# Order of the sums in the first quad of values, earlier rotary tables, and the first weight sums on VectorE

## The chip, the cores and the metric

The kernel runs on one core of a Trainium2 chip. The metric is the device time of one execution in microseconds (us); less is better. The engines are TensorE (PE: matmuls; PEld is its weight load), VectorE (DVE), ScalarE (ACT), GpSimd (POOL) and SyncE (SP, which here only issues loads). Each engine works through its own list of instructions in order and waits at an instruction until its operands and buffers are ready. DMA writes issued by POOL, and loads issued by SP, stand in those lists too.

## The reference, cut to what matters

A decoder block over 1024 positions of width 1024. The change touches its front, where the normed input is projected:

```
h    = rms_norm(x, pre_mix_norm)
proj = h @ w_in
xr, gr, q, k, v, gates = split(proj)
ang  = positions[..., None] * inv_freq          # rotary tables
cos, sin = cos(ang), sin(ang)
q = partial_rope(q, cos, sin) * 128 ** -0.5     # first 32 of 128 columns of each head
k = partial_rope(k, cos, sin)
...                                             # recurrence, dilated attention, merge, FFN
```

The values `v` come in three groups of 512 columns, since the attention has three dilations.

## The kernel before, in words

**Precision by splitting.** Every f32 operand of a product is split into a high part (ACT copies it to the matmul's type) and a low part (DVE subtracts the high part from the original). Three matmuls then stand for one: high x high, high x low, low x high (`mm3`, lines 133 to 135). A product can start when its high parts are there, and its second matmul wants the low part of the weight (values) or its third (projections).

**Seven products for eight.** Products are done as a 2 x 2 block scheme with seven block products (a "quad"). With a11, a12, a21, a22 the four blocks of a weight and b11, b12, b21, b22 those of the transposed input, sums and differences are formed first. For the input they are t1 = b12 - b11, t2 = b22 - t1, t4 = b21 - t2, t3 = b22 - b12 (`x_diffs`), for the weights s3 = a11 - a21, a21 + a22, that less a11, and a12 less that (`v_sums`).

**Stages in the front.** First, the values of group 0 (line 463). Then `v_quad(2, ...)`, the values of group 2, and `v_quad(1, ...)`, those of group 1, each with products b11, b21 (in `v_start`), t2, t1, b22, t3, t4 in that order, each of 48 matmuls of 128x256. `out` adds up two halves on DVE (`vs`) and POOL issues the write to `vd`. Then `rope_tables` makes cosine and sine on DVE (tiles `rot`) and ACT, and POOL issues six writes to `rtd`. Then `run_quads` does the projections: for the first two quads P1 and P2 (48 matmuls of 128x512), then the bodies, P6, P5, P3, P7, P4 of 12 matmuls each. `Quad.prep` forms the weight sums `sa` and `sb` with four operations on POOL (lines 267 to 270); ACT and DVE split them.

**What sets the order.** A scheduler orders each engine's list by the order in the program, by dependencies and by the ends that its own cost table gives; `tc.issue_after(i)` holds a block's instructions on an engine behind `i`. Buffers come from pools: the tag `x` has ten of [128, 1024] f32, for the input blocks and later for `vr`, `vp1`, `vu`, `vw` and `rot`; a tile gets one when its first write is placed, and waits for one to come free. t1, t3 and t4 are written over input blocks; t2 has two tiles of its own (`x2`). `wraw` has two buffers, `whi` and `wlo` three, `w0r` two.

Of the kernel before, what the change touches and what calls it, by code (L numbers as in the profile page):

```python
# [30 lines left out]
PRE1 = 2  # L31
# [31 lines left out]
def block(ctx, tc, a, out):  # L63
    nc = tc.nc
    V, A, G, T = nc.vector, nc.scalar, nc.gpsimd, nc.tensor
# [25 lines left out]
    def f(t):  # L91
        return t.bitcast(F32)
# [80 lines left out]
    last_dve = [None]  # L173
# [59 lines left out]
    class Quad:  # L233
# [25 lines left out]
            self.w = {}  # L259
            self.unit(self.raw(0, name), ("P1", "P2"))  # L260

        def prep(self):
            r0, r1 = self.raw(0), self.raw(1)
            lo_, hi_ = slice(0, 512), slice(512, 1024)
            sa = Quad.pool.tile([128, 1024], F32, name="sa")
            sb = Quad.pool.tile([128, 1024], F32, name="sb")
            G.tensor_add(sb[:, lo_], r1[:, lo_], r1[:, hi_])  # L267
            G.tensor_sub(sa[:, lo_], sb[:, lo_], r0[:, lo_])  # L268
            G.tensor_sub(sa[:, hi_], r0[:, lo_], r1[:, lo_])
            G.tensor_sub(sb[:, hi_], r0[:, hi_], sa[:, lo_])  # L270
            if self.w is None:
                self.w = {}
                self.unit(r0, ("P1", "P2"))
            self.unit(sa, ("P6", "P7"))
            self.unit(sb, ("P5", "P3"))
            h4 = Quad.pool.tile([128, 512], F32R, name="w4h", bufs=Quad.W4)
            l4 = Quad.pool.tile([128, 512], F32R, name="w4l")
            split(r1[:, hi_], h4, l4)
            self.w["P4"] = h4, l4
# [44 lines left out]
                self.done()  # L324
            yield

    def run_quads(quads, pre, tick=None):
        quads[0].prep()
        for j in range(pre):
            quads[j].first()  # L330
        for j, q in enumerate(quads):
            if j + 1 < len(quads):
                quads[j + 1].prep()
            for _ in q.body():
                if tick:
                    tick()
            if pre <= j + 1 < len(quads):
                quads[j + 1].head()
                if tick:
                    tick()  # L340
                quads[j + 1].first()
                if tick:
                    tick()
# [46 lines left out]
        return xf.tile(list(shape), F32, name=name, tag="x", bufs=10)  # L390

    X = [xq("x", (128, 2, 512)) for _ in range(10)]
    xt = dict(zip(((1, 2), (1, 3), (2, 0), (2, 1), (0, 0), (0, 1), (1, 0), (1, 1), (0, 2), (0, 3)), X))
    x2 = [xt[2, j] for j in range(2)]

    def pair(ts, j, h):

# [82 lines left out]
        for pr in range(2):  # L480
            G.dma_start(v_block(pr, 0, h), vs[:, :, 256 * pr:256 * pr + 256])

    def x_diffs(j):

        b11, b12, b21, b22 = (xt[h, 2 * u + j] for u in range(2) for h in range(2))
        V.tensor_sub(b11, b12, b11)
        V.tensor_sub(x2[j], b22, b11)
        V.tensor_sub(b21, b21, x2[j])
        V.tensor_sub(b12, b22, b12)

    for j in range(4):
        x_load(0, j)
# [61 lines left out]
    def x_split(n, src):  # L554
        for j in range(2):
            c = slice(2 * j, 2 * j + 2)
            A.activation(X1[n][0][:, c], src[j], AF.Copy)
            V.tensor_sub(X1[n][1][:, c], src[j], f(X1[n][0][:, c]))

    def x_sums(t, fl, x2c, X, names):  # L560

# [23 lines left out]
    def rope_tables():  # L585

        whole = [xq("rot") for _ in range(3)]
        pos_i, ang, nn, nh, tmp = (whole[i // 2][:, 384 * (i % 2):384 * (i % 2) + 384] for i in range(5))
        pos_i = pos_i.bitcast(I32)
        pos = a["positions"]  # L590
        A.dma_start(pos_i.rearrange("p (g n) -> p g n", g=NG),
                    bass.AP(tensor=pos.tensor, offset=pos.offset, ap=[[384, 8], [0, 16], [1, 384]]))
        V.tensor_copy(ang, pos_i)
        c1, c2, c3 = two_pi_parts()
        MAGIC = 1.5 * 2 ** 23
        V.tensor_scalar(ang, ang, cst[:, C_INV:C_INV + 1], None, op0=OP.mult)
        V.tensor_scalar(nn, ang, 1.0 / (2 * math.pi), MAGIC, op0=OP.mult, op1=OP.add)
        V.tensor_scalar(nn, nn, -MAGIC, None, op0=OP.add)
        V.tensor_scalar(nh, nn, 2.0 ** -11, MAGIC, op0=OP.mult, op1=OP.add)
        V.tensor_scalar(nh, nh, -MAGIC, 2.0 ** 11, op0=OP.add, op1=OP.mult)  # L600
        V.tensor_sub(tmp, nn, nh)
        for cc, parts in ((c1, (nh, tmp)), (c2, (nh, tmp)), (c3, (nn,))):
            for part in parts:
                V.scalar_tensor_tensor(ang, part, -cc, ang, op0=OP.mult, op1=OP.add)
        V.tensor_scalar(ang, ang, -math.pi, math.pi, op0=OP.max, op1=OP.min)
        V.scalar_tensor_tensor(tmp, ang, -1.0, ang, op0=OP.mult, op1=OP.min)
        V.tensor_scalar(tmp, tmp, math.pi / 2, None, op0=OP.add)
        A.activation(nn, ang, AF.Sin)
        A.activation(nh, tmp, AF.Sin)
        for s, src in ((0, nh), (1, nn)):  # L610
            for g in range(NG):
                G.dma_start(rtd[g, s].rearrange("f (b n) -> b f n", b=8), src[:, 128 * g:128 * g + 128])


    def v_mm(w, n):
        wh, wl = (t.rearrange("p (k n) -> p k n", n=256) for t in w)
        xh, xl = X1[n]
        bk = [ps("pv") for _ in range(2)]
        for q in range(4):
            mm3(bk[q // 2][:, 256 * (q % 2):256 * (q % 2) + 256],  # L620
                [(xh[:, k, 128 * q:128 * q + 128], xl[:, k, 128 * q:128 * q + 128], wh[:, k, :], wl[:, k, :])
                     for k in range(4)])
        return bk

    def v_split(src):
        hi = wp.tile([128, 1024], F32R, name="whi", tag="whi")
        lo = wp.tile([128, 1024], F32R, name="wlo", tag="wlo")
        A.activation(hi, src, AF.Copy)
        last_dve[0] = V.tensor_sub(lo, src, f(hi))
        return hi, lo  # L630
# [3 lines left out]

    def v_raw(g):
        r = [None] * 5
        for n in (2, 3, 0, 4, 1):
            if g == 1:
                r[n] = xq("vr")
            elif n in (2, 3):  # L640
                r[n] = w0p.tile([128, 1024], F32, name="vr", tag="w0r")
            elif n == 1:
                r[n] = xq("vr")
            else:
                r[n] = wraw()
            if n < 4:
                load(r[n], a["w_v"][n // 2, g - 1, n % 2])
        return r

    def v_sums(r):  # L650
        a11, a12, a21, a22, s3 = r
        V.tensor_sub(s3, a11, a21)
        V.tensor_add(a21, a21, a22)
        V.tensor_sub(a11, a21, a11)
        last_dve[0] = V.tensor_sub(a12, a12, a11)

    def v_quad(g, b, nxt, r, late=()):
        def add2(name, bk, x, y=None):
            if y is None:
                y = xq(name)  # L660
            for n, c in enumerate((LO, HI)):
                V.tensor_add(y[:, c], bk[n], x[:, c])
            return y

        def out(pr, u, bk, x):
            t = vp.tile([128, 4, 256], F32, name="vs")
            add2(None, bk, x, t.rearrange("p q n -> p (q n)"))
            G.dma_start(vd[pr, g, 512 * u:512 * u + 512].rearrange("(q p) n -> p q n", p=128), t)

        a11, a12, a21, a22, s3 = r  # L670
        p1 = xq("vp1")
        for n, c in enumerate((LO, HI)):
            A.activation(p1[:, c], b[0][n], AF.Copy)
        out(0, 0, b[1], p1)
        late = list(late)

        def split_and(src):
            w = v_split(src)
            if late:
                late.pop(0)()  # L680
            return w

        u2 = add2("vu", v_mm(split_and(a11), "t2"), p1)
        w = add2("vw", v_mm(split_and(a21), "t1"), u2)
        out(0, 1, v_mm(split_and(a12), "b22"), w)
        bk = v_mm(v_split(s3), "t3")
        out(1, 1, bk, w)
        v = add2("vw", bk, u2)
        b2 = v_mm(v_split(a22), "t4")
        if nxt:  # L690
            nb = v_start(nxt)
        out(1, 0, b2, v)
        return nb if nxt else None

    b = v_start(2)
    r = v_raw(2)
    v_sums(r)
    x_diffs(0)
    x_diffs(1)
    x_split("t2", x2)  # L700
    put(1, 2)
    put(1, 3)
    def x_late(n, x):
        def go():
            with tc.issue_after(last_dve[0].ins):
                x_split(n, x)

        return go

    b = v_quad(2, b, 1, r, (x_late("t1", [xt[0, 0], xt[0, 1]]), x_late("t3", [xt[1, 0], xt[1, 1]]),  # L710
                            x_late("t4", [xt[0, 2], xt[0, 3]])))
    r = v_raw(1)
    v_sums(r)
    v_quad(1, b, None, r)
    rope_tables()


    kinds = {n: dp.tile([8, 128, S], F32, name=n + "d") for n in ("xr", "gr", "gl", "ga")}
# [370 lines left out]
        todo.setdefault(c, []).append((yl_weights, (nb,)))  # L1089
    for n, (fn, args) in enumerate(EARLYA):  # L1090
        todo.setdefault(fn, []).append((after, args))
    run_quads(q1, PRE1, tick)
    assert not todo
    fctx.close()
    tctx.close()
# [509 lines left out]
```

## Time and profile before

| | before |
|---|---|
| runs (3) | 1737.4, 1739.75, 1740.69 us; median 1739.75 |
| profiled execution | 1737.8 us, of which the span from first to last instruction 1736.0 |
| PE busy | 1676.3 us, 97% of the span |
| DVE, ACT, POOL busy | 65%, 42%, 40% |
| mean granted TensorE clock | 0.982 of full speed |

PE is nearly always busy, so the time is set by its work and by the few places where it waits or where its clock is lower. Matmuls overlap, and their ends are modelled, so a matmul's row of 0.28 us doesn't mean that the next starts 0.28 us later; progress is read from the starts, or from a count over a stretch.

### The profile page before, as it was taken

Reading aid. Unit: us, or ns where it says so; the run is one execution under the profiler, and the core shown is the slowest. Engines: PE = TensorE matmul, PEld = TensorE weight load, DVE = VectorE, ACT = ScalarE, POOL = GpSimd, SP = SyncE. Lnnn points to the kernel's source line nnn. Section 1 sums busy time; section 2 is a strip of 40 time slices with the busy share of each in tenths; the row PEclk is TensorE's granted clock in tenths of the full one; section 3 lists DMA queues with packets and bytes.
Section 4 is the critical chain, followed back from the end, with each engine's and each line's share of the span. In section 5 each row is a group of like instructions: output and inputs, shape, how many; then the busy total and the mean of one; then the engine's idle time right before and its main releaser. Section 6 shows DMA issues by size and latency. Waiting matters only on the chain.

```text
span 1736.0 us, 21088 instructions
## 1 busy us (share of the span) xinstructions
PE 1676.3 (97%) x7748; PEld 1376.8 (79%) x7748; DVE 1121.0 (65%) x1591; ACT 728.4 (42%) x1130; POOL 693.2 (40%) x644
## 2 busy tenths in 40 slices
PE   9999999999999999989999999799999999999996
PEld 7897888787877887868888787678888888788885
DVE  7956577778887766554433678755554555659658
ACT  6423367564555532564441445323222222345343
POOL 2003454554445533133334205576566666400103
PEclk9999999999999999999999999899999999999998
DMA  8233433343333564683519742133222222475353
GB/s 322 85 123 123 146 128 130 131 149 118 128 133 134 167 206 156 229 317 135 195 50 359 245 147 73 61 123 126 103 91 103 92 96 105 160 255 191 109 188 121
DMA packets 95919, 262.70 MB, mean 151 GB/s; under 512 B 13768, under 2 KB 22120, under 8 KB 94408
## 3 DMA queue, kind: packets, MB, share of 16 engines
q1 hardware_dynamic: 70352, 182.49, 31.2%
q0 software_dynamic: 20352, 76.21, 11.6%
q10 hardware_dynamic: 5112, 2.66, 0.5%
q8 instruction: 61, 1.00, 0.2%
q14 instruction: 42, 0.34, 0.1%
HBM read 180.86 MB, written 80.35 MB: 150 GB/s over the span
## 4 chain that ended last, share of the span: by engine, by line
PE 77%; DVE 10%; DMA 4%; issue 4%; POOL 3%; ACT 3%; SPq 0%; ACTq 0%; DVEq 0%; POOLq 0%
PE pq L135 15%; PE pq L134 15%; PE pq L133 15%; PE pd L1351 4%; PE pd L1352 4%; PE pd L1350 4%; PE py L135 2%; PE py L133 2%; PE py L134 2%; PE pv L463 2%; PE po L1033 2%; PE pv L134 1%; PE pv L135 1%; DMA rsn<-rtd 1%; PE pv L133 1%
## 5 line engine op out<-in xcount | busy, mean ns | idle before, releaser
L133 PE MATMUL pq<-hth,whi 128*128 128x512 f32 x448 | 179.3, 400 | 2.7 <-ACT whi L98 2.7
L135 PE MATMUL pq<-hth,wlo 128*128 128x512 f32 x448 | 178.5, 399 | 3.1 <-DVE wlo L99 3.1
L134 PE MATMUL pq<-htl,whi 128*128 128x512 f32 x448 | 180.5, 403 | 0.0
L267 POOL TENSOR_TENSOR sb<-wraw 128x512 f32<-128x512 f32 x50 | 70.9, 1418 | 168.3 <-DMA wraw<-in_w_fg 92.1
L98 ACT ACTIVATE whi<-sa 128x1024 fp32r<-128x1024 f32 x50 | 52.9, 1059 | 198.6 <-PE pq L134 139.4
L1351 PE MATMUL pd<-fbl,fah 128*128 128x512 f32 x304 | 119.6, 394 | 4.5 <-DVE fbl L99 4.5
L1352 PE MATMUL pd<-fbh,fal 128*128 128x512 f32 x304 | 119.7, 394 | 0.0
L1350 PE MATMUL pd<-fbh,fah 128*128 128x512 f32 x304 | 119.4, 393 | 0.0
L99 DVE TENSOR_TENSOR wlo<-wraw,whi 128x1024 fp32r<-128x1024 f32 x67 | 97.5, 1456 | 23.6 <-ACT whi L98 20.8
L98 ACT ACTIVATE whi<-wraw 128x1024 fp32r<-128x1024 f32 x67 | 70.7, 1056 | 90.8 <-PE pq L134 26.3
L309 DVE TENSOR_TENSOR uw<-pq,uw 128x512 f32<-128x512 f32 x100 | 68.4, 684 | 57.6 <-PE pq L135 56.8
L133 PEld LDWEIGHTS pq<-hth,whi 128*128 128x128 f32 x448 | 85.8, 191 | 24.7 <-ACT whi L98 3.2
L135 PEld LDWEIGHTS pq<-hth,wlo 128*128 128x128 f32 x448 | 85.5, 191 | 24.3 <-DVE wlo L99 3.8
L134 PEld LDWEIGHTS pq<-htl,whi 128*128 128x128 f32 x448 | 85.7, 191 | 20.3
L1424 POOL TENSOR_TENSOR y<-y,gpf 128x512 f32<-128x512 f32 x16 | 26.2, 1663 | 186.0 <-ACT fah L98 109.7
L99 DVE TENSOR_TENSOR wlo<-sa,whi 128x1024 fp32r<-128x1024 f32 x50 | 70.1, 1402 | 27.7 <-ACT whi L98 27.7
L728 DVE TENSOR_TENSOR fb<-pq,uw 128x512 f32<-128x512 f32 x84 | 67.8, 807 | 30.6 <-PE pq L135 30.3
L1256 POOL TENSOR_TENSOR fo<-fo,ut 128x512 f32<-128x512 f32 x44 | 60.6, 1381 | 66.4 <-DVE ut L1255 66.4
L98 ACT ACTIVATE fah<-ar 128x1024 fp32r<-128x1024 f32 (+1 forms) x41 | 40.8, 995 | 98.6 <-PE pd L1351 76.5
L99 DVE TENSOR_TENSOR fal<-ar,fah 128x1024 fp32r<-128x1024 f32 (+1 forms) x41 | 49.3, 1203 | 48.7 <-ACT fah L98 48.6
L268 POOL TENSOR_TENSOR sa<-sb,wraw 128x512 f32<-128x512 f32 x50 | 80.2, 1604 | 0.0
L133 PE MATMUL pq<-t1h,whi 128*128 128x512 f32 x200 | 79.4, 397 | 0.5 <-ACT whi L98 0.5
(541 smaller groups left out, 4946.9 us busy)
## 6 DMA issues: line engine op xcount, KB each, us to landing
ar<-fd SPq DMA_DIRECT2D x35, 512.0 KB
qkd<-fb POOLq DMA_DIRECT2D x24, 512.0 KB, 3.6
qk<-qkd SPq DMA_DIRECT2D x24, 512.0 KB
wraw<-in_w_fg SPq DMA_DIRECT2D x24, 512.0 KB
wraw<-in_w_fu SPq DMA_DIRECT2D x24, 512.0 KB
fd<-fo POOLq DMA_DIRECT2D x11, 1024.0 KB, 4.3
wd<-in_w_dn SPq DMA_DIRECT2D x21, 512.0 KB
fd<-fs POOLq DMA_DIRECT2D x11, 768.0 KB, 5.6
```

Of the source, the lines that this page charges most:

```text
L98: A.activation(hi, src, AF.Copy)
L99: (le or V).tensor_sub(lo, src, f(hi))
L133: T.matmul(o, lh, rh, start=(first and i == 0), stop=False)
L134: T.matmul(o, lh, rl, start=False, stop=False)
L135: T.matmul(o, ll, rh, start=False, stop=(last and i == n - 1))
L267: G.tensor_add(sb[:, lo_], r1[:, lo_], r1[:, hi_])
L268: G.tensor_sub(sa[:, lo_], sb[:, lo_], r0[:, lo_])
L309: V.tensor_add(y, bank, x)
L728: V.tensor_add(o, half_in(bank, g), half_in(add, g))
L1350: T.matmul(o, ah[:, ts], bh, start=(i == 0), stop=False)
L1351: T.matmul(o, ah[:, ts], bl, start=False, stop=False)
L1352: T.matmul(o, al[:, ts], bh, start=False, stop=(i == NP - 1))
```

## The change

In the first quad of values, `x_diff` and `v_sums` now run in the order in which the products want them: t1 and t2, then the weight sums for the first two products, splits of t2 and of a11, of t1, and then t3; the last weight sum (`v_sum4`, a12) and t4 come during the quad. The raw blocks are loaded in the order a21, a11, a22, a12. Two small memsets write one column of t2's tiles at the start, so that they get their buffers there. `rope_tables` stands ahead of the last quad of values, and its six writes are issued by SP (cosine) and ACT (sine) instead of POOL. `run_quads` gets `V`, so that the first projection quad's four sums run on DVE.

```diff
-        def prep(self):
+        def prep(self, first=None):
...
-            G.tensor_add(sb[:, lo_], r1[:, lo_], r1[:, hi_])
-            G.tensor_sub(sa[:, lo_], sb[:, lo_], r0[:, lo_])
-            G.tensor_sub(sa[:, hi_], r0[:, lo_], r1[:, lo_])
-            G.tensor_sub(sb[:, hi_], r0[:, hi_], sa[:, lo_])
+            E = first or G
+            E.tensor_add(sb[:, lo_], r1[:, lo_], r1[:, hi_])
+            E.tensor_sub(sa[:, lo_], sb[:, lo_], r0[:, lo_])
+            E.tensor_sub(sa[:, hi_], r0[:, lo_], r1[:, lo_])
+            E.tensor_sub(sb[:, hi_], r0[:, hi_], sa[:, lo_])
...
-    xt = dict(zip(((1, 2), (1, 3), (2, 0), (2, 1), (0, 0), (0, 1), (1, 0), (1, 1), (0, 2), (0, 3)), X))
+    xt = dict(zip(((0, 0), (0, 1), (1, 2), (1, 3), (2, 0), (2, 1), (1, 0), (1, 1), (0, 2), (0, 3)), X))
     x2 = [xt[2, j] for j in range(2)]
+    for x in x2:
+        V.memset(x[:, 0, 0:1], 0.0)
...
-    def x_diffs(j):
...
+    def x_diff(n):
+
+        for j in range(2):
+            b11, b12, b21, b22 = (xt[h, 2 * u + j] for u in range(2) for h in range(2))
+            o, p, q = dict(t1=(b11, b12, b11), t2=(x2[j], b22, b11), t4=(b21, b21, x2[j]), t3=(b12, b22, b12))[n]
+            last_dve[0] = V.tensor_sub(o, p, q)
...
-                G.dma_start(rtd[g, s].rearrange("f (b n) -> b f n", b=8), src[:, 128 * g:128 * g + 128])
+                (A if s else nc.sync).dma_start(rtd[g, s].rearrange("f (b n) -> b f n", b=8), src[:, 128 * g:128 * g + 128])
...
-        for n in (2, 3, 0, 4, 1):
+        for n in (2, 0, 3, 4, 1):
...
-        V.tensor_sub(a11, a21, a11)
-        last_dve[0] = V.tensor_sub(a12, a12, a11)
+        last_dve[0] = V.tensor_sub(a11, a21, a11)
+
+    def v_sum4(r):
+        V.tensor_sub(r[1], r[1], r[0])
...
-    v_sums(r)
-    x_diffs(0)
-    x_diffs(1)
-    x_split("t2", x2)
-    put(1, 2)
-    put(1, 3)
...
+    x_diff("t1")
+    x_diff("t2")
+    with tc.issue_after(last_dve[0].ins):
+        v_sums(r)
+    with tc.issue_after(last_dve[0].ins):
+        x_split("t2", x2)
+    with tc.issue_after(last_dve[0].ins):
+        w1 = v_split(r[0])
+    with tc.issue_after(last_dve[0].ins):
+        x_split("t1", [xt[0, 0], xt[0, 1]])
+        put(1, 2)
+        x_diff("t3")
+        put(1, 3)
+    early = last_dve[0].ins
...
+    b = v_quad(2, b, 1, r, (late_a12, late_t3, late_t4), w1)
     r = v_raw(1)
     v_sums(r)
+    v_sum4(r)
+    rope_tables()
     v_quad(1, b, None, r)
-    rope_tables()
...
-    run_quads(q1, PRE1, tick)
+    run_quads(q1, PRE1, tick, V)
```

**First place: DVE ahead of the t2 product of the first quad.** In the kernel before, x_126 and x_127 are the halves of t2, x_130 and x_131 of t3, wraw_621 the block a11, vr_624 the block a12; htl0 takes low parts of t2, htl1 of b22.

```order
L654 TENSOR_TENSOR wraw_621<-vr_617,wraw_621 128x1024
L489 TENSOR_TENSOR x_131<-x_125,x_131 128x1024
L655 TENSOR_TENSOR vr_624<-vr_624,wraw_621 128x1024
L558 TENSOR_TENSOR htl0_122<-x_126,hth0_120 128x2x512
L426 TENSOR_TENSOR htl1_123<-x_124,hth1_121 128x2x512
L487 TENSOR_TENSOR x_127<-x_125,x_129 128x1024
L426 TENSOR_TENSOR htl1_123<-x_125,hth1_121 128x2x512
L488 TENSOR_TENSOR x_133<-x_133,x_127 128x1024
L558 TENSOR_TENSOR htl0_122<-x_127,hth0_120 128x2x512
L662 TENSOR_TENSOR vs_649<-pv_567,vp1_646 128x512
L662 TENSOR_TENSOR vs_649<-pv_568,vp1_646 128x512
L629 TENSOR_TENSOR wlo_654<-wraw_621,whi_653 128x1024
```

In the changed kernel x_124 and x_125 are t1, x_128 and x_129 t2, wraw_625 is s3, vr_619 the block a21 and vr_623 the block a22.

```order
L491 TENSOR_TENSOR x_124<-x_130,x_124 128x1024
L491 TENSOR_TENSOR x_125<-x_131,x_125 128x1024
L491 TENSOR_TENSOR x_128<-x_126,x_124 128x1024
L491 TENSOR_TENSOR x_129<-x_127,x_125 128x1024
L654 TENSOR_TENSOR wraw_625<-wraw_621,vr_619 128x1024
L655 TENSOR_TENSOR vr_619<-vr_619,vr_623 128x1024
L656 TENSOR_TENSOR wraw_621<-vr_619,wraw_621 128x1024
L560 TENSOR_TENSOR htl0_122<-x_128,hth0_120 128x2x512
L560 TENSOR_TENSOR htl0_122<-x_129,hth0_120 128x2x512
L631 TENSOR_TENSOR wlo_640<-wraw_621,whi_639 128x1024
L429 TENSOR_TENSOR htl1_123<-x_126,hth1_121 128x2x512
L560 TENSOR_TENSOR t1l1_502<-x_124,t1h1_501 128x1024
```

Both halves of t2 and the low part of a11 moved ahead of the sums of t3, t4 and a12 and ahead of the evacuations `vs`.

**Second place: DVE ahead of the t1 product of the first quad, changed kernel.** These rows follow the last ones; vr_619 is a21, x_130 and x_131 are t3, and `vu` is the sum u2.

```order
L560 TENSOR_TENSOR t1l1_502<-x_125,t1h1_501 128x1024
L491 TENSOR_TENSOR x_130<-x_126,x_130 128x1024
L491 TENSOR_TENSOR x_131<-x_127,x_131 128x1024
L429 TENSOR_TENSOR htl1_123<-x_127,hth1_121 128x2x512
L666 TENSOR_TENSOR vs_656<-pv_569,vp1_653 128x512
L666 TENSOR_TENSOR vs_656<-pv_570,vp1_653 128x512
L666 TENSOR_TENSOR vu_710<-pv_660,vp1_653 128x512
L631 TENSOR_TENSOR wlo_714<-vr_619,whi_713 128x1024
```

The sums of t3 and the evacuations now lie between the low parts of t1 and that of a21; before, the sums of t3 were done long ahead and t1's low parts came behind the evacuations.

**Third place: the tables and the first weight sums.** POOL's list before, at the end of the values:

```order
L668 DMA vd<-vs 128x4x256 x8
L612 DMA rtd<-rot 8x16x128 x6
L267 TENSOR_TENSOR sb<-wraw 128x512
L269 TENSOR_TENSOR sa<-wraw 128x512
L268 TENSOR_TENSOR sa<-sb,wraw 128x512
L270 TENSOR_TENSOR sb<-wraw,sa 128x512
```

ACT's list in the changed kernel, from the evacuations of the last quad's b11 to the first weights of the projections:

```order
L677 ACTIVATE vp_1110<-pv 128x512 x2
L630 ACTIVATE whi<-vr 128x1024
L610 ACT_TABLE_LOAD
L610 ACTIVATE rot<-rot 128x384
L614 DMA rtd<-rot 8x16x128
L611 ACTIVATE rot<-rot 128x384
L614 DMA rtd<-rot 8x16x128 x2
L630 ACTIVATE whi<-vr 128x1024 x2
L356 ACT_TABLE_LOAD
L356 ACTIVATE lv<-lv 128x8
L98 ACTIVATE whi<-wraw 128x1024 x2
```

DVE's list in the changed kernel, at the end of the values:

```order
L666 TENSOR_TENSOR vs<-pv,vw 128x512 x2
L268 TENSOR_TENSOR sb<-wraw 128x512
L270 TENSOR_TENSOR sa<-wraw 128x512
L269 TENSOR_TENSOR sa<-sb,wraw 128x512
L99 TENSOR_TENSOR w4l<-wraw,w4h 128x512
L271 TENSOR_TENSOR sb<-wraw,sa 128x512
L99 TENSOR_TENSOR wlo<-sa,whi 128x1024
```

The first four sums left POOL's list, where they stood behind six table writes, for DVE's, behind the last evacuation; ACT's two sines and three of the writes now stand ahead of the splits of the last quad's s3 and a22.

## Rows read from the trace of the kernel before

**Rows 1.** Waits of PE, 60 to 80 and 150 to 162 us: who, for whom, total, times, longest.
```profile
PE pv L133 <- ACT whi L628: 1.8, 1, 1.8
PE pv L134 <- DVE wlo L629: 1.2, 1, 1.2
...
PE pq L133 <- ACT whi L98: 3.2, 2, 2.7
```

**Rows 2.** Stretches: length, busy us (instructions) of PE, PEld, DVE, ACT, POOL, clock, DMA.
```profile
55.44:66.71 11.27, 11.27 (x98) 11.26 (x96) 11.27 (x11) 9.01 (x12) 1.45 (x2) 1.00 0.28 93
66.71:74.91 8.20, 5.25 (x29) 4.83 (x28) 7.23 (x8) 4.23 (x5) 0.79 (x1) 0.79 0.43 130
...
140.10:151.25 11.15, 11.15 (x50) 8.79 (x48) 4.70 (x12) 1.71 (x4) 6.43 (x9) 1.00 0.28 87
151.25:160.23 8.98, 5.79 (x13) 3.97 (x13) 5.16 (x5) 4.97 (x6) 4.07 (x4) 0.62 0.34 117
...
153.40:160.00 6.60, 5.40 (x12) 3.81 (x13) 3.01 (x3) 3.66 (x4) 1.77 (x2) 0.50 0.47 159
```

**Rows 3.** Timeline of DVE: start, duration in us, instruction.
```profile
49.87 2.35 DVE L486 TENSOR_TENSOR x<-x 128x1024 f32<-128x1024 f32 x2
...
63.49 1.22 DVE L487 TENSOR_TENSOR x<-x 128x1024 f32<-128x1024 f32 x1
...
68.33 1.28 DVE L662 TENSOR_TENSOR vs<-pv,vp 128x512 f32<-128x512 f32 x2
69.53 1.22 DVE L629 TENSOR_TENSOR wlo<-wraw,whi 128x1024 fp32r<-128x1024 f32 x1
...
98.15 1.21 DVE L652 TENSOR_TENSOR vr<-vr 128x1024 f32<-128x1024 f32 x1
99.40 1.23 DVE L653 TENSOR_TENSOR vr<-vr 128x1024 f32<-128x1024 f32 x1
```

**Rows 4.** The chain that ended last, 144 to 156 us: start, duration, what.
```profile
144.95 0.54 ACT rot L609
...
145.77 1.70 POOL rtd L612 x3
...
148.14 2.23 DMA rtd<-rot
...
150.49 1.29 POOL sa L269
...
153.07 1.61 POOL sb L270
...
154.71 1.06 ACT whi L98
```

**Rows 5.** Timeline of ACT, 61 to 64 us.
```profile
61.34 1.06 ACT L628 ACTIVATE whi<-vr 128x1024 fp32r<-128x1024 f32 x1 [1.15 <-PE pv L135]
62.30 1.99 ACT L557 ACTIVATE t1h<-x 128x1024 fp32r<-128x1024 f32 x2
```

**Rows 6.** Timeline of SP's queue: issues of loads.
```profile
48.84 0.33 SPq L109 DMA_DIRECT2D wraw<-in_w_v  x1
49.22 0.42 SPq L109 DMA_DIRECT2D vr<-in_w_v  x1
...
131.27 6.33 SPq L109 DMA_DIRECT2D wraw<-in_w_gr  x2
```

**Rows 7.** Stretch 53 to 54 us, columns as in rows 2 (last: GB/s).
```profile
53.00:54.00 1.00, 1.00 (x6) 0.83 (x5) 1.00 (x2) 0.37 (x1) 0.00 (x0) 1.00 0.02 8
```

**Rows 8.** Timeline of DVE and ACT: first rotary operation, and the first sine.
```profile
135.77 0.35 DVE L593 CAST rot<-rot 128x384 f32<-128x384 int32 x1
...
143.97 0.53 ACT L608 ACTIVATE rot<-rot 128x384 f32<-128x384 f32 x1 [6.99 <-DVE rot L605]
```

**Rows 9.** One tile's operations (ns, minimum/median/maximum), and timeline of DVE at 152 us.
```profile
L825 DVE TENSOR_TENSOR rm<-rq,rsn x6: 683/692/834, 595.1 to 675.6; 128x512 f32<-128x512 f32 x6
...
152.43 1.12 DVE L99 TENSOR_TENSOR w4l<-wraw,w4h 128x512 fp32r<-128x512 f32 x1
```

More of the change, by code (lines that the diff above doesn't have):

```diff
@@ L325, in body, with run_quads @@
             yield
-    def run_quads(quads, pre, tick=None):
-        quads[0].prep()
+    def run_quads(quads, pre, tick=None, first=None):
+        quads[0].prep(first)
         for j in range(pre):
@@ L481, in v0_out @@
             G.dma_start(v_block(pr, 0, h), vs[:, :, 256 * pr:256 * pr + 256])
-    def x_diffs(j):
[L485 to L489, printed above, removed]
+    def x_diff(n):
[3 more added lines that the diff above has]
+            last_dve[0] = V.tensor_sub(o, p, q)
     for j in range(4):
@@ L557, in x_split @@
             A.activation(X1[n][0][:, c], src[j], AF.Copy)
-            V.tensor_sub(X1[n][1][:, c], src[j], f(X1[n][0][:, c]))
+            last_dve[0] = V.tensor_sub(X1[n][1][:, c], src[j], f(X1[n][0][:, c]))
     def x_sums(t, fl, x2c, X, names):
@@ L653, in v_sums, with v_quad @@
         V.tensor_add(a21, a21, a22)
-        V.tensor_sub(a11, a21, a11)
-        last_dve[0] = V.tensor_sub(a12, a12, a11)
-    def v_quad(g, b, nxt, r, late=()):
+        last_dve[0] = V.tensor_sub(a11, a21, a11)
+    def v_sum4(r):
+        V.tensor_sub(r[1], r[1], r[0])
+    def v_quad(g, b, nxt, r, late=(), w1=None):
         def add2(name, bk, x, y=None):
@@ L681, in split_and @@
             return w
-        u2 = add2("vu", v_mm(split_and(a11), "t2"), p1)
+        u2 = add2("vu", v_mm(w1 or split_and(a11), "t2"), p1)
         w = add2("vw", v_mm(split_and(a21), "t1"), u2)
         out(0, 1, v_mm(split_and(a12), "b22"), w)
-        bk = v_mm(v_split(s3), "t3")
+        bk = v_mm(split_and(s3), "t3")
         out(1, 1, bk, w)
@@ L696, in block, with late_a12, late_t3, late_t4 @@
     r = v_raw(2)
-    v_sums(r)
-    x_diffs(0)
-    x_diffs(1)
-    x_split("t2", x2)
-    put(1, 2)
-    put(1, 3)
[L703 to L711, printed above, removed]
+    x_diff("t1")
[12 more added lines that the diff above has]
+    early = last_dve[0].ins
+    def late_a12():
+        with tc.issue_after(last_dve[0].ins):
+            v_sum4(r2)
+    def late_t3():
+        with tc.issue_after(last_dve[0].ins):
+            x_split("t3", [xt[1, 0], xt[1, 1]])
+    def late_t4():
+        with tc.issue_after(early):
+            x_diff("t4")
+            x_split("t4", [xt[0, 2], xt[0, 3]])
+    r2 = r
+    b = v_quad(2, b, 1, r, (late_a12, late_t3, late_t4), w1)
     r = v_raw(1)
     v_sums(r)
+    v_sum4(r)
+    rope_tables()
     v_quad(1, b, None, r)
-    rope_tables()
     kinds = {n: dp.tile([8, 128, S], F32, name=n + "d") for n in ("xr", "gr", "gl", "ga")}
```

## The prediction

> **What bounds the kernel now.** I first read who TensorE (PE) waited for. Between 40 and 300 us only two places count: in the first quad of values PE waits 1.8 us for a high part made by ScalarE (ACT) and 1.2 us for a low part made by VectorE (DVE), and at the start of the projections 3.2 us for the high parts of the first weight sums [rows 1]. Everywhere else in that stretch PE is full, so time can be saved there only.
>
> A wait costs more than its idle time, so I take the loss from PE's progress [rows 2]. From 55.44 to 66.71 PE runs two products of 48 matmuls of 128x256: 11.27/96 = 0.117 us each. From 66.71 to 74.91 it touches 29 matmuls, of which two began earlier: 27 x 0.117 = 3.17 us of work in 8.20 us, **loss A = 5.03 us**. From 140.10 to 151.25 it touches 50 matmuls of 128x512, two begun earlier: 11.15/48 = 0.232 us each. From 151.25 to 160.23 it touches 13, one begun earlier: 12 x 0.232 = 2.79 us of work in 8.98 us, **loss B = 6.19 us**. Part of each is clock: the mean granted clock is 0.79 and 0.62 in the two stretches, and 0.50 (1.2 GHz instead of 2.4) from 153.40 to 160.00, after PE had stood since 151.25 [rows 2].
>
> What is late in A: DVE. It works without a gap, but its list holds the sums of x and of weights in mixed order; the second half of "t2" is written only at 63.49, and the low part of a11, the product's weight, at 69.53, behind two evacuations at 68.33 [rows 3]. What is late in B: the chain that ended last runs through the rotary tables: the second sine on ACT at 144.95, POOL's table writes from 145.77, the landing of a write at 148.14, and then POOL's weight sums of 1.29 to 1.61 us each, ACT's split of sb at 154.71, and PE [rows 4]. The sums stand behind the writes in POOL's queue and their buffers are those that the tables give free.
>
> **First quad, in the order of its products.** The sums, splits and their count stay (8 of x, 4 of weights); only order and buffers change. Independent DVE operations of 128x1024 follow each other at 2.35 - 1.22 = 1.13 us (two take 2.35 in the row at 49.87, one 1.22); where one needs the one before, 99.40 - 98.15 = 1.25 us [rows 3]. The new list from 49.87: t1 twice, t2 twice, s3 at 54.4, a21 at 55.6, a11 at 56.9, low parts of t2 at 58.0 and 59.2, low part of a11 at 60.3 to 61.5. PE comes to the t2 product at 66.71. Margin 5.2 us; A as it was is gone.
>
> What is late next: the t1 product. It begins at 66.71 + 5.64 = 72.35 and wants the low part of a21 with its second matmul, 72.47. DVE's list goes on: low part of b22 at 61.45; then t1's low parts, which need ACT. ACT can split a21 only when PE gives a buffer free, at 61.34, and t1 from 62.30 [rows 5], so t1's low parts start at 63.4 and 64.5. Then two t3 sums, one low part, two evacuations and one sum of u2 (0.60 each, by the 1.28 that two take at 68.33), and a21's low part from 70.9 to 72.1. Margin 0.35 us, the thinnest of all. I price it at 0; the bounds are 0 and one more operation in front, 1.22 us.
>
> After that the same count gives b22's weight low part ready at 76.1 for 77.98 (margin 1.9), s3's at 80.8 for 83.6 (2.8), a22's at 86.6 for 89.3 (2.7). Price 0 while these hold.
>
> **Its loads.** a22 was fetched early, before a11; now it stands behind a11 on SP, which waits for a buffer until 48.84. So a22 takes the place of a12, issued at 49.22 [rows 6]. That pair's traffic is over by 53 us (8 GB/s from 53.00) [rows 7], and DVE wants a22 for a21's sum at 55.6: margin 2.6, price 0. Each us beyond it would push the whole list, and after 0.35 more the t1 product. a12 now waits for a buffer that t1 gives free, about 64.6; with the 4.2 us that the pair took for both it is there by 68.8, wanted at 72.1. Queued behind it on SP are the next quad's first weights: issued near 73.2, landed by 77.4, wanted by PE at 94.9. The two 128x1 memsets that claim the t2 buffers lie at the start, behind the memset on which PE waits; a bound is the shortest rotary operation of 128x384, 0.35 us each [rows 8], and DVE then waits for loads anyway: 0.
>
> **Rotary tables earlier.** Their 16 DVE operations took from 135.77 to the sine at 144.95, 9.2 us with three others between [rows 4, 8]. They now lie within the last quad of values, where the same count leaves DVE over 5 us ahead of PE: 0. Six table writes leave POOL's queue; three go to SP, where the next load is due some 15 us later, three to ACT, ahead of its last two weight splits. Price 0 with the margin given under the slower rival.
>
> **First weight sums on DVE.** PE reaches the first product of the projections at 151.25 - 5.03 = 146.22. The second raw weight was issued at 131.27 + 6.33 - 0.33 = 137.27 [rows 6]; 5.03 earlier is 132.2, landed by 136.4 at the pair's 4.2 us. A sum of 128x512 with both inputs in SBUF takes DVE 0.69 us [rows 9]; the third completes sa at 138.5; ACT's split 1.06 us: 139.7; DVE's low part 1.22: 140.9. Margin over 5 us: loss B is gone. If all four sums met POOL they would take longer: a DVE operation of this size took 1.12 us at 152.43 beside POOL's sum [rows 9]. Even with a whole POOL operation of 1.29 [rows 4] in front of each, sa is complete at 136.4 + 3 x 1.98 = 142.3 and its low part by 145. POOL's own next sums come when the next raw weights land, near 144, for a product at 146.2 + 14 = 160.
>
> The Trainium skill, "SBUF — State Buffer", section "Who interferes with whom", says that a DVE operation with two SBUF inputs and a GpSimd operation that reads SBUF exclude each other, the later one blocking in full. By that rule the trace's 1.12 us is 0.69 plus the rest of the POOL sum, and it agrees; the rule speaks against moving sums onto DVE where POOL sums on. By it the moved sums would cost up to the 1.98 us each just used, which still lies in the margin.
>
> **The sum.** 1737.8 (the profiled execution: its span of 1736.0 and 1.8 around it) - 5.03 - 6.19 = 1726.6 us. Behind 160 us the program is as before, and everything in it is triggered by what comes ahead, so the gain should not be given back. The profiled execution lies 1.95 us under the median of 1739.75; from the median the sum is 1728.5. I say 1727.5, between.
>
> **Rivals.**
> *Remainder in the first quad* (0.10): a21's low part, or a22's load, is late and PE waits up to 1.2 us, with no fall of the clock to speak of: 1726.6 to 1728. For it: a margin of 0.35. Against: all that stands before it is counted from rows.
> *Sums collide* (0.03): the port rule above bites harder than I count, for instance on the splits' low parts as well: some 1 us of B stays, 1727.6.
> *Only one loss goes* (0.08): A goes and B stays (projections' raw weights land 5 us later than counted): 1732.8; or B goes and A only moves to another product: 1731.6.
> *Nothing comes of it* (0.05): both waits are replaced by others of their size, 1737.8. The order lists speak against it: the operations did move.
> *Slower* (0.03): ACT is blocked behind the tables. Its sine waited 6.99 us for DVE's chain [rows 8]; in the change two weight splits of the last quad (s3, a22) and two table writes are queued behind that sine. The chain should start near 98 (the last quad's sums began at 98.15, now 5 earlier, with 4 x 1.25 us of sums) and, with some 3.5 us of others in it, end near 111. PE wants s3's low part ten products after 66.71, at 66.71 + 56.4 + 0.1 = 123.2; less the low part's 1.22, the split's 1.06 and about one us for the two writes, the sine must be done by about 120. From 9 us late on, each us costs one, and from about 20 us late (131) it eats both gains: above 1737.8, say 1740 at 133.
>
> **How the numbers follow.** The forecast that both losses go has 0.71, and the rivals as given. Measured from no change I count 0.2% (3.5 us) as what can be told. Faster: 0.71 + 0.10 + 0.03 + 0.08 = 0.92; same 0.05; slower 0.03. The forecast's own range is 1725 to 1730 (1726.6 to 1728.5, the unknown 1.2, and half the spread of the runs, 1.6). To leave out no more than 2 in 10 it must reach the cases with one loss: 1724 to 1733.
>
> **What would show it.** Right: in the stretch 66 to 92 us PE without a gap and at clock 1.00; the t1 product near 72.4; the evacuations of the t2 product and of all after it some 5 us earlier; the first weight sums on DVE near 136 us at 0.69 each; PE at clock 1.00 through 140 to 160 and the projections some 11 us earlier. Wrong: a wait of PE at 72.4 for the low part of a21 over 1.2 us; DVE waiting near 55.6 for a22; ACT waiting past 120 for the tables; PE waiting near 146 for ACT's split of sa; or the same 11 us lost again further back.

## The result and the profile after

| | before | changed |
|---|---|---|
| runs | 4, 1733.08 to 1740.69 us, median 1738.58 | 4, 1720.44 to 1724.68 us, median **1723.16** |
| ratio | | 0.9915, 95% interval 0.9893 to 0.9936 |
| span of the profiled execution | 1736.0 us | 1718.6 us |
| PE busy; mean granted clock | 1676.3 us; 0.982 | 1663.9 us; 0.988 |

The change is faster by 14.8 us by the ratio (11.1 to 18.6), where 1727.5 us and a range of 1724 to 1733 were forecast. The time came out 0.84 us under that range.

The same stretches as in [rows 2], of the changed kernel (length, busy us and instructions of PE, PEld, DVE, ACT and POOL, clock, DMA share, GB/s):

```profile
55.44:66.71 11.27, 11.27 (x98) 11.27 (x97) 10.49 (x10) 8.36 (x11) 1.46 (x2) 1.00 0.38 121
66.71:74.91 8.20, 8.20 (x73) 8.20 (x72) 8.20 (x11) 3.88 (x5) 0.79 (x1) 1.00 0.35 111
...
140.10:151.25 11.15, 11.15 (x49) 8.99 (x48) 4.54 (x5) 4.40 (x5) 5.08 (x4) 1.00 0.32 112
151.25:160.23 8.98, 8.98 (x40) 7.23 (x40) 5.61 (x7) 3.80 (x5) 0.57 (x1) 1.00 0.15 60
```

Where PE touched 29 and 13 matmuls at a clock of 0.79 and 0.62 [rows 2], it now touches 73 and 40 at 1.00 and is busy throughout. The waits of [rows 1] are gone: from 40 to 290 us the list of PE's waits is empty.

The timeline of DVE in the changed kernel, ahead of the first quad's t2 and t1 products and at the first weight sums:

```profile
58.00 2.35 DVE L560 TENSOR_TENSOR htl<-x,hth 128x1024 fp32r<-128x1024 f32 x2
60.27 1.22 DVE L631 TENSOR_TENSOR wlo<-wraw,whi 128x1024 fp32r<-128x1024 f32 x1
...
63.34 2.36 DVE L560 TENSOR_TENSOR t1l<-x,t1h 128x1024 fp32r<-128x1024 f32 x2 [0.72 <-ACT t1h L559]
...
70.82 1.22 DVE L631 TENSOR_TENSOR wlo<-vr,whi 128x1024 fp32r<-128x1024 f32 x1
...
135.14 0.69 DVE L268 TENSOR_TENSOR sb<-wraw 128x512 f32<-128x512 f32 x1
...
136.35 0.68 DVE L269 TENSOR_TENSOR sa<-sb,wraw 128x512 f32<-128x512 f32 x1
...
138.24 1.23 DVE L99 TENSOR_TENSOR wlo<-sa,whi 128x1024 fp32r<-128x1024 f32 x1
```

The low part of a11 (the row at 60.27) stood at 69.53 before [rows 3]; that of a21, on the thinnest margin, is made from 70.82 to 72.04, and PE needs it at 72.42. The sums take 0.69 us each, and the low part of sa is done at 139.5, some 6 us before PE wants it. On ACT and SP's queue the tables are out of the way early; before, the first sine stood at 143.97 [rows 8]:

```profile
108.72 0.53 ACT L610 ACTIVATE rot<-rot 128x384 f32<-128x384 f32 x1
...
110.51 2.13 SPq L614 DMA_DIRECT2D rtd<-rot  x3
```

**Where the 17.4 us of the two spans lie.** I matched the matmuls of the two traces one by one. Up to 65.5 us they start at the same time (within 0.1 us). Behind the first quad's stall the changed kernel leads by 5.13 us, just before the projections by 5.78, behind the second stall by 11.95. So the front gave what was forecast and 0.7 more, and the rest, some 5 us, came far behind all that the change touches.

### The profile page after: what moved, and what is told of

Its sections match the earlier page's. It is cut to its first block, busy times and chain, and to the rows that moved or that the text cites. A ratio compares the mean times of both kernels' runs of the same rounds, so it can differ in the third digit from the quotient of the medians.

```text
span 1718.6 us, 21094 instructions
## 1 busy us (share of the span) xinstructions
PE 1663.9 (97%) x7748; PEld 1368.1 (80%) x7748; DVE 1120.0 (65%) x1597; ACT 728.9 (42%) x1130; POOL 683.3 (40%) x634
## 4 chain that ended last, share of the span: by engine, by line
PE 77%; DVE 9%; DMA 4%; issue 4%; ACT 2%; POOL 2%; SPq 1%; ACTq 0%; DVEq 0%; POOLq 0%
PE pq L135 15%; PE pq L134 15%; PE pq L133 15%; PE pd L1371 3%; PE pd L1372 3%; PE pd L1370 3%; PE py L135 2%; PE py L133 2%; PE py L134 2%; PE pv L466 2%; PE po L1053 2%; PE pv L134 2%; PE pv L135 2%; PE pv L133 2%; DMA rsn<-rtd 1%
## 5 line engine op out<-in xcount | busy, mean ns | idle before, releaser
L134 PE MATMUL pq<-t1l,whi 128*128 128x512 f32 x200 | 78.9, 395 | 0.0
```

The source lines that it names most:

```text
L134: T.matmul(o, lh, rl, start=False, stop=False)
```

## The experiments

Theory 1: the change gives the two forecast losses, near 12 us in all, and what else was measured is the luck of an execution, above all how often the clock falls behind waits that both kernels have. Theory 2: the change makes later work shorter. A second question is which part of the change took the second loss away. Each group of runs shared its chip and its runs of the kernel before.

**Both kernels again, and the change in halves.** Run e1 is the changed kernel as it is, e2 the kernel before. Run e3 keeps the first quad and takes back the rest:

```diff
-    rope_tables()
     v_quad(1, b, None, r)
+    rope_tables()
...
-                (A if s else nc.sync).dma_start(rtd[g, s]...
+                G.dma_start(rtd[g, s]...
...
-    run_quads(q1, PRE1, tick, V)
+    run_quads(q1, PRE1, tick)
```

Run e4 is the kernel before with the first two of these hunks the other way round: the tables alone.

> The change, repeated in five rounds. Theory 1 (the two losses of the front are worth 11.2 to 12 us; what the first measurement showed beyond that comes from how far TensorE's clock falls behind stalls that both kernels have, and that differs from run to run): ratio to the kernel before nearer to 0.993 (12 us) than to 0.9915, and in the new profile the losses behind the unchanged stalls near 415, 540, 1492 and 1680 us differ from those of the first profile (5.6, 2.8, 2.7, 2.3 us) by up to 1.6 us each. Theory 2 (the change also shortens those later losses for good): ratio again 0.991 or less, and the same small losses at the same places.

> The kernel before, unchanged, against itself. Both theories: ratio 1.000 within 0.2%. Theory 1: its new profile shows other losses behind the later stalls than the first one (6.8 us near 426, 3.9 near 553, 4.3 near 1507, 3.8 near 1697), some of them as small as with the change. Theory 2: the same large losses at all four places.

> The first quad's new order alone; tables and first weight sums as before. Theory 1: the stall near 67 us is gone (5.0 us, and some 0.7 us more because the products behind it take 5.63 instead of 5.70 us), the one before the projections stays at 6.2 us: 5 to 6 us under the kernel before. Theory 2: more than 7 us.

> Rotary tables ahead of the last quad of values, their writes on SP and ACT; first quad as before, first weight sums on POOL. If POOL's queue behind the table writes is the whole cause of the loss before the projections, that loss (6.2 us) is gone without moving the sums: 6 us under the kernel before, first sums on POOL near 137 us. If POOL's slower sums matter (four of 1.3 us instead of 0.7), TensorE still waits there for sa or sb, and less than 4 us is gained.

| run | median us | ratio to before (1738.03) |
|---|---|---|
| e1, change again | 1725.13 | 0.9923 (0.9909 to 0.9936) |
| e2, before again | 1737.69 | 0.9998 (0.9988 to 1.0007) |
| e3, first quad alone | 1731.25 | 0.9960 (0.9947 to 0.9972) |
| e4, tables alone | 1732.59 | 0.9966 (0.9953 to 0.9978) |

e1's ratio lies midway between what the two theories expected, and its interval holds both; its profile is as theory 1 had it, with 0.8 to 1.6 us more lost at each of the four later stalls that the expectation names than in the first profile. In e2 only the last of the four losses is smaller than in the first profile of the kernel before, by 1.6 us. But e6 below, which at these four places is the kernel before, loses 1.2 to 1.6 us less there at each, as little as the changed kernel's first profile. So a loss there is small or large with the execution, not with the change.

The halves give 6.8 and 5.4 us by their medians, 12.2 in sum, against 12.9 for the whole: they add up, as far as intervals of some 2 us each way can tell. e3's 6.8 lies between the ranges of its two theories, so its time doesn't decide; its trace does. PE's waits from 40 to 170 us, of e3 and then of e4 (who, for whom, total, times, longest):

```profile
PE pq L133 <- ACT whi L98: 3.3, 2, 2.3
```

```profile
PE pv L133 <- ACT whi L628: 1.8, 1, 1.8
PE pv L134 <- DVE wlo L629: 1.2, 1, 1.2
```

Each half removes its own wait and leaves the other as in [rows 1]. And e4 has no wait before the projections although its sums are on POOL. e4 moves the tables and has their writes issued by other engines; the two were not tried apart.

**Are the sums on VectorE needed?** Run e5, and e10 once more, is the change with `run_quads(q1, PRE1, tick)`, without `V`; e9 is the change a third time, beside e10. Run e11 is the kernel before with only `prep(first)` and `V`; e12 is e4 with them.

> The change, with the first four weight sums of the projections left on POOL. Theory 1 (what gave the second gain is that the tables and their writes no longer stand ahead of these sums; the move to VectorE adds nothing, as the tables-alone run had no wait there with its sums on POOL): no PE wait for ACT's whi at 140 to 160 us, PE at clock 1.00 there, and the time of the change, 1723 to 1725.5 us, ratio to the change 0.999 to 1.001. Theory 2 (the sums had to leave POOL): a wait of 1 to 3 us comes back near 146 us and the time is 2 to 6 us above the change's.

> The change as it is, a third time, beside the run with the sums on POOL. Theory 1: 12 to 15 us under the kernel before, ratio 0.9915 to 0.993, and up to 160 us the same rows as in the other two profiles of the change; the losses behind 160 us differ from those two by the clock behind waits of the same length.

> The change with the first four weight sums of the projections on POOL, again, on the same chip as the change itself; the first time it was 9.4 us under the kernel before against 12.9 for the change, with no wait of PE in 140 to 160 us. Theory 1 (the move of the sums adds nothing to the time): within 1.5 us of the change beside it. Theory 2 (it adds something further back that the first profile didn't show): 3 to 5 us above it.

> The kernel before, with only the first four weight sums of the projections on VectorE; tables late, their writes on POOL, first quad as it was. Theory 1 (the sums' buffers are those that the tables give free, so the sums wait for the table writes on whichever engine they stand): PE still waits 2 to 3.3 us near 151 us, and the time is that of before, 0 to 2 us less. Theory 2 (it was POOL's 1.29 to 1.61 us each and its queue): the wait is gone, 5 to 6 us faster, ratio 0.9966.

> The kernel before, with the tables ahead of the last quad of values and the first sums on VectorE; first quad as it was. The tables alone gave 5.4 us, without a wait of PE before the projections. Theory 1 (the sums add nothing to that): 5 to 6.5 us under before, ratio 0.9963 to 0.9971, PE without a wait in 140 to 160 us. Theory 2 (the sums add something of their own): 8 to 10 us, ratio 0.994 to 0.9955.

| run | median us | ratio to before |
|---|---|---|
| e5, sums on POOL | 1728.34 | 0.9946 (0.9931 to 0.9961), before 1736.64 |
| e10, the same again | 1725.51 | 0.9927 (0.9914 to 0.9940), before 1737.83 |
| e9, change third | 1727.09 | 0.9931 (0.9917 to 0.9945), before 1737.83 |
| e11, sums alone | 1735.15 | 0.9984 (0.9975 to 0.9993), before 1737.83 |
| e12, tables and sums | 1731.01 | 0.9963 (0.9951 to 0.9975), before 1737.83 |

Taken alone, e5 looked like a cost of some 3.5 us for sums on POOL (9.4 us under the kernel before, against 12.9 in e1): it missed the time that theory 1 gave it, though the wait that theory 2 named isn't there. Beside the change on one chip (e9, e10) the difference is 1.6 us the other way, and e12 equals e4 within the noise. Once the tables are early, moving the sums adds nothing that these runs can tell. Without early tables it adds 2.7 us (1.2 to 4.3; I had expected 0 to 2). The timeline of DVE in e11:

```profile
144.62 0.68 DVE L268 TENSOR_TENSOR sb<-wraw 128x512 f32<-128x512 f32 x1
150.32 0.69 DVE L270 TENSOR_TENSOR sa<-wraw 128x512 f32<-128x512 f32 x1 [5.02 <-DMA rtd<-rot]
150.93 0.69 DVE L269 TENSOR_TENSOR sa<-sb,wraw 128x512 f32<-128x512 f32 x1
...
153.22 1.22 DVE L99 TENSOR_TENSOR wlo<-sa,whi 128x1024 fp32r<-128x1024 f32 x1
```

The sum of sa stands for 5.02 us until a table write has landed, since it gets the tables' buffer: as theory 1 had it, the sums wait for the tables on whichever engine they are. Then 0.69 us instead of 1.29 [rows 4] shortens PE's waits to 2.5 us in all, and the clock holds behind them (1.00 from 149 to 162 us; in the kernel before 0.74).

Sums on POOL are not free for DVE, they only miss PE. In e5, DVE and then POOL:

```profile
135.96 4.68 DVE L99 TENSOR_TENSOR w4l<-wraw,w4h 128x512 fp32r<-128x512 f32 x1 [0.72 <-ACT w4h L98]
...
141.22 1.66 DVE L99 TENSOR_TENSOR wlo<-sa,whi 128x1024 fp32r<-128x1024 f32 x1 [0.56 <-ACT whi L98]
```

```profile
136.31 1.30 POOL L268 TENSOR_TENSOR sb<-wraw 128x512 f32<-128x512 f32 x1
137.56 1.29 POOL L270 TENSOR_TENSOR sa<-wraw 128x512 f32<-128x512 f32 x1
138.81 1.28 POOL L269 TENSOR_TENSOR sa<-sb,wraw 128x512 f32<-128x512 f32 x1
140.17 1.63 POOL L271 TENSOR_TENSOR sb<-wraw,sa 128x512 f32<-128x512 f32 x1
```

The same `w4l` takes 0.68 us in the changed kernel. Here it lasts until three POOL sums in a row are over, and so it does in e10 (4.55 us) and e4 (4.41). The low part of sa is there at 142.9, still 3 us ahead of PE, which needs it near 146.

**What of a loss is idle time, what is clock?** In run e6, the kernel before, useless matmuls stand where PE waits; their results go nowhere.

```diff
...
+    def fill(n, lh, rh):
+        o = ps("fill")
+        for i in range(n):
+            with tc.issue_after(last_pe[0].ins):
+                last_pe[0] = T.matmul(o, lh, rh, start=True, stop=True)
...
+        if g == 2:
+            fill(11, X1["b21"][0][:, 0, 0:128], X1["b21"][0][:, 0, :])
         u2 = add2("vu", v_mm(split_and(a11), "t2"), p1)
...
+        if tick:
+            fill(12, Quad.X["b21"][0][:, 0, 0:128], Quad.X["b21"][0][:, 0, :])
         for j, q in enumerate(quads):
```

> The kernel before, with 11 useless matmuls of 128x512 ahead of the t2 product of the first quad and 12 ahead of the first P6 of the projections, where PE stood for 2.95 and 3.19 us; nothing else is moved and no result is used. Theory 1 (of the losses of 5.03 and 6.19 us only the idle time is the wait's, and the other 2.1 and 3.0 us are the lower clock behind it, which comes because PE stands): the stretches 66 to 76 and 150 to 161 us stay at clock 1.00, the two losses fall to about 3.0 and 3.2 us, and the kernel is 5.1 us faster than before, ratio 0.997. Theory 2 (the clock falls for another reason, or the waits only move by the time of the added matmuls): no change, or up to 5.5 us slower.

Measured: 1736.03 us, ratio 0.9990 (0.9978 to 1.0001): 1.7 us faster, with an interval from none to 3.8, where I expected 5.1. The stretches around the two stalls, in e6 and then in the kernel before:

```profile
66.50:77.00 10.50, 9.79 (x73) 9.14 (x73) 10.29 (x12) 4.89 (x6) 0.79 (x1) 1.00 0.34 101
149.00:162.00 13.00, 11.97 (x51) 9.08 (x50) 6.63 (x7) 5.70 (x7) 7.87 (x7) 1.00 0.23 82
```

```profile
66.50:77.00 10.50, 7.55 (x49) 7.13 (x48) 9.09 (x10) 4.44 (x5) 0.79 (x1) 0.84 0.33 101
149.00:162.00 13.00, 9.81 (x31) 7.03 (x30) 5.88 (x6) 5.63 (x7) 7.66 (x6) 0.74 0.26 88
```

The clock stays at its upper level (2.4 GHz), as theory 1 said. Without the 11 and 12 added ones PE does 62 matmuls in place of 49 and 39 in place of 31. What is left of the losses is 3.5 us (11 x 0.233 added, 0.95 lost) and 4.3 us (12 x 0.233 and 1.54), 7.8 of 11.2 us. So with the clock up 3.4 us less is lost in this profile, and not 5.1. Run e4, whose first quad is that of the kernel before with nothing added, shows the same for the first stall:

```profile
66.50:77.00 10.50, 7.54 (x62) 7.13 (x62) 10.29 (x11) 4.88 (x6) 0.79 (x1) 1.00 0.33 101
```

PE waits 1.76 and 1.20 us there as well, the clock stays at 1.00 all the same, and the loss is 3.5 us. So the clock can stay up behind such waits without filling, and some 0.5 us of what I had put down to the clock in the first loss is lost with the clock up too.

**Filling two late waits.** In e7 the change, in e8 the kernel before, gets 9 and 8 such matmuls in two waits for `fbl` of the last projection, which no part of the change touches.

```diff
-    def down(bk, t, i, w):
+    def down(bk, t, i, w, n=0):
...
+        if n:
+            fill(n, ah[:, ts], bh)
...
-                    down(banks, t, i, w)
+                    down(banks, t, i, w, {0: 9, 37: 8}.get(n, 0) if t == k == 0 else 0)
```

> The change, with 9 useless matmuls of 128x512 in the wait of PE for fbl near 1493 us and 8 in the one near 1681 us; both waits (2.44 and 2.06 us) are in the kernel before too, and cost 2.69 and 2.32 us in one profile of the change, 4.25 and 3.81 us in another, where the clock fell behind them. Theory 1 (what came in beyond the two forecast losses, and what differs between runs of one kernel, is the clock behind waits that the change doesn't touch): both spots cost 2.2 to 2.8 us in the profile, with the clock at 1.00 behind them; the time is 0.5 to 3 us under the change's, and its difference to the kernel before with the same filling is 11 to 13 us. Theory 2 (the change itself makes later work shorter): the difference stays at 14 to 16 us.

> The kernel before, with the same filling of the two late waits as in the run above it. Theory 1: 0.5 to 3 us under the kernel before, 1735 to 1737.5 us, and both spots cost 2.2 to 2.8 us. Theory 2: the same here too, but 14 to 16 us above the filled change.

| run | median us | ratio to before (1736.64) |
|---|---|---|
| e7, change, late waits filled | 1723.29 | 0.9925 (0.9909 to 0.9942) |
| e8, before, late waits filled | 1735.52 | 0.9997 (0.9988 to 1.0006) |

Between the two lie 12.2 us by the medians, inside theory 1's 11 to 13 and under theory 2's 14 to 16. But the five runs of e7 spread over 4.4 us and the eleven of e8 over 5.3, so the 12.2 is uncertain by about 2 us and doesn't rule out 14 (the two profiled spans, one execution each, lie 14.6 apart). The filling itself gave some 1 us in e8, at the low end of what was expected; for e7 it can't be read, since no unfilled change ran beside it. The two spots cost 2.9 and 2.3 us in e7 and 3.0 and 2.3 in e8, the added matmuls included, where 2.2 to 2.8 were expected: the added matmuls take much of the time that they save. The stretch behind the first of these waits, in the first profile of the change, in e1 (the same kernel) and in e7:

```profile
1490.00:1503.00 13.00, 10.56 (x47) 8.43 (x46) 11.84 (x7) 7.26 (x7) 9.88 (x7) 1.00 0.78 260
```

```profile
1493.00:1506.00 13.00, 10.56 (x39) 8.21 (x39) 11.68 (x7) 6.85 (x7) 9.59 (x7) 0.87 0.81 252
```

```profile
1493.00:1506.00 13.00, 12.35 (x55) 9.91 (x54) 11.61 (x7) 6.95 (x7) 9.51 (x7) 1.00 0.80 258
```

In the first two, PE waits for the same 2.44 us and is busy for the same 10.56 us. Once the clock stays at 1.00 and 47 matmuls are done, once it is 0.87 in the mean and 39 are done.

**The change against itself.** The start of the same matmul of PE, in the kernel before and in the three profiles of the change; in brackets how far it leads:

| place | before | change | e1 | e9 |
|---|---|---|---|---|
| gate products | 426.49 | 414.57 (11.9) | 414.78 (11.7) | 414.82 (11.7) |
| late projections | 657.63 | 643.76 (13.9) | 646.19 (11.4) | 646.06 (11.6) |
| attention | 931.13 | 915.74 (15.4) | 918.00 (13.1) | 921.85 (9.3) |
| last projection, first wait | 1507.44 | 1492.59 (14.9) | 1495.31 (12.1) | 1498.97 (8.5) |
| its second wait | 1696.76 | 1680.28 (16.5) | 1684.62 (12.1) | 1688.19 (8.6) |
| span | 1736.0 | 1718.6 (17.4) | 1723.3 (12.7) | 1726.9 (9.1) |

To 415 us all three lead alike. Then they part by up to 8 us, and the one that the result shows drew the best of it. From there to the end the lead changes by +5.4, +1.0 and -2.6 us, and in e5 and e10 by +1.5 and -2.0: 0.7 in the mean of the five. One such place is the late projections, where PE waits for a low part that DVE makes behind a rotary load (`rsn`). SP's issue and DVE's operation on what landed, in the first profile of the change and then in e9:

```profile
630.12 0.57 SPq L109 DMA_DIRECT2D rsn<-rtd  x1
...
640.39 0.69 DVE L845 TENSOR_TENSOR rm<-rq,rsn 128x512 f32<-128x512 f32 x1 [8.67 <-DMA qkd<-rq]
```

```profile
632.63 0.57 SPq L109 DMA_DIRECT2D rsn<-rtd  x1
644.96 0.69 DVE L845 TENSOR_TENSOR rm<-rq,rsn 128x512 f32<-128x512 f32 x1 [10.73 <-DMA rsn<-rtd]
```

From the issue to the operation it takes 10.3 us once, where the row names the write of `rq` as what came last, and 12.3 the other time, where it names the load; PE's wait is 2.9 us and 5.2. At the last projection's two waits e9 and e1 lost some 4.2 and 3.8 us by the starts of the matmuls, the first profile 2.7 and 2.3.

## Why the prediction was right in its steps and its range was not

**Loss A** (forecast 5.03 us): 5.13, and e3 shows that the first quad alone takes it away. The order worked as counted: a21's low part at 70.82 to 72.04, forecast 70.9 to 72.1, and the t1 product met no wait on its margin of 0.35. The loads' margins held too: the block a12 was issued at 64.6 and the next weights at 73.20, as forecast.

**Loss B** (forecast 6.19 us): 6.17. What took it away is the tables' new place with their writes on other engines, shown by e4, e10 and e12. The price of 0 for the tables held, with the second sine at 109.96 where the end of their chain was put near 111.

**The port rule.** That a DVE operation is held up by POOL's sums is shown more strongly by e5 than I allowed for. I let one POOL operation stand in front of each moved sum, 1.98 us; e5 has three in front of one, 4.68. The Trainium skill, "SBUF — State Buffer", section "Who interferes with whom", has the two exclude each other and the later one blocked in full. e5's rows agree that they exclude each other (`w4l` ends 0.55 us behind the third POOL sum), but not on which is held up: the row of `w4l` begins 0.35 us before the first POOL sum's, in e10 0.20 and in e4 0.05 before it (POOL's rows are rough), and yet it waits for three. In the change itself the two don't meet, and that rival fell, as did the three in which a loss stayed and the slower one: DVE's sums end at 138.2, and POOL's next begin at 142.83.

**What failed** is the end of the sum: "Behind 160 us the program is as before, and everything in it is triggered by what comes ahead, so the gain should not be given back", with "half the spread of the runs, 1.6" as all that the far part could add to the range. The far part was put at nothing: in the result's profile it added 5.4 us to the lead, in e1 1.0, and in e9 it took 2.6 away. The gain of the front is not given back as a rule, and the order of each engine's operations behind 170 us is the same in both traces. But the far part is no constant: the runs of the kernel before alone lie within 1732.4 and 1741.6 us, and the medians of the very same changed kernel were 1723.16, 1725.13 and 1727.09, with ratios of 0.9915, 0.9923 and 0.9931. The forecast of 1727.5 lies above all three, and the low end of 1724 between the first two. That the result fell under it is for the most part the luck of its executions. The low end had no case of its own either: the cases with one loss, for which the range was widened, lie on its upper side. A range with the 4 us by which medians of one kernel differ, in place of 1.6 us, would have held all three. The base of the sum was some 1 us high as well: 1727.5 and the two losses make 1738.7, while the medians of the kernel before in the later groups are 1736.64 to 1738.03.

**A smaller miss** is 0.65 us between the two losses, not forecast at all. The stretch from 80 to 100 us, products of 48 matmuls of 128x256, in the kernel before, in the changed one, and in e12:

```profile
80.00:100.00 20.00, 20.00 (x171) 20.00 (x170) 14.61 (x18) 3.19 (x3) 1.52 (x2) 1.00 0.66 232
```

```profile
80.00:100.00 20.00, 20.00 (x173) 20.00 (x173) 18.82 (x23) 4.25 (x4) 2.27 (x3) 1.00 0.76 274
```

```profile
80.00:100.00 20.00, 20.00 (x169) 20.00 (x168) 14.37 (x17) 3.18 (x3) 1.52 (x2) 1.00 0.67 231
```

PE is busy throughout at clock 1.00 in all three, and yet does 171, 173 and 169: by the starts, a product takes 5.70, 5.63 and 5.76 us. In the seven profiles without the first stall it is 5.63; in those with it 5.70 (before, e2, e11), 5.76 (e12) or 5.63 (e4, e8, and e6 with its shortened stall). So the next ten products were 1 to 2% slower in four of the seven profiles with the stall and in none of the seven without. That the stall is the cause, and how, is not shown.

**What stays open** beside that: what decides whether the clock falls behind a wait of given length, and which part of the first quad's new order would do alone.

Nor is it so that nothing of the change reaches the work behind 415 us. Near 756 us PE waits for a high part of ACT (`lTh`) 2.07 to 2.28 us in the four profiles with the front of the kernel before, filled or not (before, e2, e6, e8), and 0.92 to 1.13 us in the six of the change (with the sums on either engine, filled or not). The next wait, for `qk`, is longer in those six (4.9 to 5.4 us against 3.2 to 3.9) and takes part of it back. From 743 to 777 us the lead grows by 0.5 to 0.8 us in the six, and falls by 0.2 to 0.4 in e2, e6 and e8. In the parts of the change taken alone it grows by 0.3 to 0.7 (e4, e11, e12) or falls by 0.5 (e3). So some 0.9 us of the later gain goes with the change, although no operation there has another place in its engine's list. Why is not shown.

## What to carry to other kernels

Read a stall's cost from the engine's progress, and look for what stands ahead of the late operation in its engine's list: sums in the order of their products, and the tables out of the way of the first weight sums, gave both losses back in full. Of two edits aimed at one wait, test each alone: here early tables did all of it, and moving the sums nothing more that these runs could tell. And before giving a range, ask what the unchanged part does from one execution to the next; a gain read to 0.1 us in the traces stands in a time that moves by 4 us.

## What the runs showed of the hardware

- The same wait of 2.44 us costs 2.7 or 4.25 us in different profiles of one kernel (by the starts of the matmuls), as the granted clock stays at 1.00 or falls behind it. The first quad's stall, with the same two waits of 1.76 and 1.20 us, cost 3.5 us in e4 and 6.0 in e8 (mean granted clock from 66.5 to 77 us: 1.00 and 0.67).
- With useless matmuls in the wait the granted clock was 1.00 in all four places where they were tried (six stretches of e6, e7 and e8), but it was 1.00 in e4's stall without them too. The time fell by 1.7 us in e6 (interval from none to 3.8).
- A VectorE operation of 0.68 us took 4.68, 4.55 and 4.41 us (e5, e10, e4) beside three GpSimd sums in a row, and its row begins before the first of them.
- Matmuls of one shape, with PE busy throughout and the clock at 1.00, ran at three paces some 1% apart (5.63, 5.70 and 5.76 us for 48 matmuls of 128x256).
